# A hybrid mLSTM and neighbourhood-attention layer: key transposes spread over three steps, gate rows woven into a projection, eleven kinds of stores issued by ScalarE

## The chip, the core and the metric

The kernel runs on one core of a Trainium2 chip. The metric is the device time of one execution in microseconds, as the median of several runs. Before the change it is 1791.4 us (three runs: 1791.37, 1791.40, 1798.38).

## What is computed

One encoder layer over two sequences, a prompt of 512 tokens and a sample of 2048, each with 16 learned meta tokens in front, model width 1024, all in float32. RMS norm, one combined input projection, two branches with a SiLU gate each, one output projection into the residual. Branch A is a bidirectional mLSTM (4 heads of 128, one scan per direction), branch B neighbourhood attention over a grid of 64 columns (8 heads of 64, a window of 8 x 16 keys and the meta tokens). Cut to what matters here:

```python
def hybrid_layer(h, norm_g, w_in, b_gate, conv_w, mlstm_norm_g, q_norm_g, k_norm_g, rpb, w_out):
    proj = rms_norm(h, norm_g) @ w_in
    q_m, k_m, v_m, o_m, z_m, gates, q_a, k_a, v_a, z_a = jnp.split(proj, cuts, axis=-1)
    qk_m = silu(centred_dwconv(concatenate([q_m, k_m]), conv_w))
    h_m = mlstm_bidir(heads(q_m), heads(k_m), heads(v_m), gates + b_gate)
    h_m = rms_norm(sigmoid(heads(o_m)) * h_m, mlstm_norm_g)
    y_m = h_m * silu(z_m)
    qa, ka = rms_norm(heads(q_a), q_norm_g), rms_norm(heads(k_a), k_norm_g)
    a = neighbourhood_attention(qa, ka, heads(v_a), rpb)   # softmax over window and meta keys
    y_a = a * silu(z_a)
    return h + concatenate([y_m, y_a]) @ w_out
```

## The kernel before

Every projection is made of float32r matmuls of 128 x 128 weights: input and weight are split into a high and a low part, and three products are summed (`mm3`, L233 to L240; the tiles `mmt` and `mmf`). The 2560 tokens are worked off in two halves of 1280, each as blocks of 256, 512 and 512 tokens. A unit of work is 24 matmuls into a PSUM buffer of the pool `ps_mm`, which has two.

The program is a row of phases that are generators. `weave` (L923) runs one main generator and lets others go on by so many steps per step of the main one; `drain` runs one to its end. In turn:

- First half: `phase_a1` projects the attention's queries, keys and values (`qs`, `ks`, `vs` in HBM), `phase_a1_z` the attention's gate (`zs`), `phase_a2` the mLSTM's inputs (`kqs`, `vms`, `ozs`). Beside `phase_a2` the first attention runs, windows 1 and 2, at 0.3 steps per step.
- Second half: `phase_a1` with the rest of the first attention (0.6). Then `gate_rows` (L529): from the gates of all tokens it makes, for each of two directions, the scan's running sums and maxima, a chain of TensorE transposes, VectorE scans and ScalarE exponentials on tiles of 84 rows, all emitted at once. Then `phase_a1_z` with the second attention, windows 3, 4 and 0 (1.2), then `phase_a2` with the attention and the backward mLSTM states (`mlstm_back`).
- Last: `mlstm`, 20 chunks of 128 tokens, each with the output projection of an earlier chunk (`out_proj`, tile `ops`).

Attention goes by pairs of heads and windows (`AttPair`, L802). One pair has four steps (`attention`, L480). Tiles: `qt`, `kt`, `vt` are loaded; `qps` and `kps` are TensorE transposes of queries and keys, copied out as `Q` (VectorE) and `K` (ScalarE); `sps` are the scores, `s` their exponentials (VectorE adds the bias, ScalarE exponentiates), `pps` the transposes of `s`, copied out as `pt` (one by ScalarE, one by VectorE); `py` sums the values, `rb` is the transposed table of softmax reciprocals (`rx`, made by POOL), and `zt` = `rb` times gate times `py` is stored in `yas`. PSUM has four pools of two buffers: `ps_mm`, `ps_a` for `sps`, `ps_b` for `kps` and `pps`, `ps_c` for `qps`, `py`, `rb` and the gate rows' tiles.

Every DMA, load or store, is issued by SP, in order: an issue that waits holds all that stand behind it. `turn` (L163) fixes TensorE's order in the woven phases as emitted; the rest of the order is made by a scheduler when the program is built. Names of stores and lines: `qs`, `ks`, `vs` L340, `kmeta`, `vmeta` L300, `zs` L375, `kqs` L423 and L443, `vms`, `ozs` L456 and L474, `Mrow` L594, `cbs` L657, outputs L799, `yas` L920.

Of the kernel before, what the change touches and what calls it, by code (L numbers as in the profile page):

```python
# [92 lines left out]
class Run:  # L93
# [4 lines left out]
    def setup(self):  # L98
# [19 lines left out]
        nc.vector.memset(self.one, 1.0)  # L118

# [156 lines left out]
    def a1_meta(self, pool, gi, w, blk):  # L276
# [22 lines left out]
        for par in range(2):  # L299
            nc.sync.dma_start(out=dst[:, par::2, gi % 2 * 256:gi % 2 * 256 + 256], in_=raw[par * 8:par * 8 + 8].unsqueeze(1).to_broadcast([8, 4, 256]))  # L300
        yield

    def a1_tokens(self, pool, gi, n, w, blk):
# [4 lines left out]
        for t0 in range(0, blk["n"] // 128, 2):  # L308
# [36 lines left out]
    def phase_a1(self, blocks, pool, first=None):  # L345
# [3 lines left out]
        if first:  # L349
            g0 = 2  # L350
            for blk in blocks:
                for gi in range(2):
                    yield from self.a1_unit(pool, gi, self.A1[gi][1], first[gi], blk)
        for gi in range(g0, 6):
            c0, n = self.A1[gi]
            w = self.load_w(a["w_in"], c0, n)
            for blk in blocks() if callable(blocks) else blocks:
                yield from self.a1_unit(pool, gi, n, w, blk)

    def phase_a1_z(self, blocks, pool, done):  # L360

        nc, a = self.nc, self.a
        for gi in range(2):
            w = self.load_w(a["w_in"], 4112 + gi * 256, 256)
            for ct in range(2):
                for blk in blocks:
# [8 lines left out]
                    nc.sync.dma_start(out=self.zs[f:f + 128, blk["row0"]:blk["row0"] + n], in_=t[:, :n])  # L375
# [28 lines left out]
    def a2_conv(self, blocks, pool, c0, cbase, gi):  # L404
        nc, a, scr = self.nc, self.a, self.kqs
        w = self.load_w(a["w_in"], c0 + gi * 256, 256)
        for ct in range(2):
# [3 lines left out]
            for blk in blocks:  # L411
# [6 lines left out]
                if extra:  # L418
                    nc.vector.tensor_copy(out=self.mraw[:, cc, 4:4 + NM], in_=ps[:, n:n + NM])
                    if cbase == 4:  # L420
                        t = self.conv(pool, self.mraw[:, cc, :], 16, cc)
                        for sq in "PS":
                            nc.sync.dma_start(out=scr[sq][f:f + 128, 0:14], in_=t[:, 2:16])  # L423
# [19 lines left out]
                nc.sync.dma_start(out=scr[s][f:f + 128, o0:o0 + no], in_=t[:, :no])  # L443
                yield

    def a2_rows(self, blocks, pool, c0, kind, gi, free=None):
# [3 lines left out]
        for blk in blocks:  # L450
            if not blk["seq"]:
                if kind == "v":
# [3 lines left out]
                    nc.sync.dma_start(out=self.vms[2560:2560 + NM, dc:dc + 256], in_=buf[:NM])  # L456
# [4 lines left out]
            for t0 in range(0, blk["n"] // 128, 2):  # L461
# [12 lines left out]
                nc.sync.dma_start(out=dst[g0:g0 + 256, d0:d0 + 256].rearrange("(t p) c -> p t c", p=128), in_=buf.rearrange("p (t c) -> p t c", t=2))  # L474
# [5 lines left out]
    def attention(self, pool, wins, zdone):  # L480
# [3 lines left out]
        todo[0].prep(0)  # L484
        yield
        todo[0].prep(1)
        yield
        prev = None
        for n, p in enumerate(todo):
# [25 lines left out]
            if after:  # L515
                after.prep(1)
# [3 lines left out]
        yield  # L520
        yield
# [4 lines left out]
        prev.out()  # L526


    def gate_rows(self, pool):  # L529
# [4 lines left out]
        misc = pool.tile([128, 8, 128], F32, tag="kt", name="gmisc", bufs=2)  # L534
        zero, ones = misc[:NR, 0, :], misc[:NR, 1, :]
        nc.vector.memset(zero, 0.0)
        nc.vector.memset(ones, 1.0)
        self.cols = cp.tile([128, 2, 4, NR], F32, name="gcols")
        for d in range(2):
            big = pool.tile([128, 8, 128], F32, tag="vt", name=f"gbig{d}", bufs=2)  # L540
            mn, t, b, a, A, M, ws, ac = (big[:NR, i, :] for i in range(8))
            E = t
            row = misc[0:1, 2 + 3 * d:5 + 3 * d, :].rearrange("p a b -> p (a b)")[:, :4 * NR].rearrange("p (i r) -> p i r", i=4)
# [12 lines left out]
            nc.vector.tensor_tensor_scan(out=rv(A), data0=rv(a), data1=rv(zero), initial=-BIG, op0=ALU.max, op1=ALU.add)  # L556
            last = slice(127, 128) if d == 0 else slice(0, 1)
# [10 lines left out]
            for c0, nch in ((0, 4), (4, 16)):  # L568
# [25 lines left out]
            nc.sync.dma_start(out=self.Mrow[d].rearrange("(r j) -> r j", r=NR), in_=M)  # L594
# [10 lines left out]
            nc.vector.tensor_copy(out=cols[:, 3, :], in_=pd[:, 0:NR])  # L605

# [38 lines left out]
    def mlstm_back(self, pool, seq):  # L645
# [4 lines left out]
        for i in range(nch - 1, 0, -1):  # L650
# [6 lines left out]
            nc.sync.dma_start(out=self.cbs[c0 + i - 1], in_=C.rearrange("p h e -> p (h e)"))  # L657
# [104 lines left out]
    def load_wo(self, pool):  # L762
# [13 lines left out]
    def out_proj(self, seq, i, yh, yl):  # L776
# [22 lines left out]
        nc.sync.dma_start(out=ydst[i * 128:(i + 1) * 128, :], in_=x)  # L799


class AttPair:  # L802
# [9 lines left out]
    def load(self):  # L812
        nc, r, pool, nr, nk, f = self.nc, self.r, self.pool, self.nr, self.nk, self.f
        self.kt = pool.tile([128, 8, 128], F32, tag="kt", name="kt", bufs=2)
        self.vt = pool.tile([128, 8, 128], F32, tag="vt", name="vt", bufs=2)
# [9 lines left out]
    def prep(self, part):  # L825
# [10 lines left out]
        for half in range(2):  # L836
            ps = r.ps_b.tile([128, 512], F32, tag="t", name="kps")
            for c in range(4):
                r.turn(nc.tensor.transpose(ps[:, c * nk:(c + 1) * nk], self.kt[:nk, half * 4 + c, :], r.ident[:nk, :nk]))
            nc.scalar.activation(out=self.K[:, half * 4 * nk:(half + 1) * 4 * nk], in_=ps[:, :4 * nk], func=AF.Copy, scale=r.gk)  # L840

    def start(self):
        pool = self.pool
        self.py = self.r.ps_c.tile([128, 512], F32, tag="c", name="py")
# [3 lines left out]
    def scores(self, b):  # L848
        nc, r, pool, nk, n, bt = self.nc, self.r, self.pool, self.nk, 3 * self.nk, BTYPE[b]
        if bt not in self.bias:  # L850
            self.bias[bt] = pool.tile([128, 2, n], F32, tag="bias", name="bias", bufs=4)
# [8 lines left out]
        for hh in range(2):  # L860
            s = pool.tile([128, 384], F32, tag="s", name="s", bufs=6)
# [22 lines left out]
    def values(self, half):  # L884

        nc, r, nk, pts = self.nc, self.r, self.nk, self.pts.pop(half)
        order = ((1, 4, 0, 2, 3), (6, 3, 7, 5, 4))[half]
# [15 lines left out]

    def out(self):
# [240 lines left out]
```

## Time and profile before

| | before |
|---|---|
| median of three runs | 1791.4 us |
| the profiled execution | 1794.23 us |
| its span in the profile | 1792.5 us |
| TensorE matmul busy | 1693.5 us, 94% |
| VectorE busy | 906.5 us, 51% |
| ScalarE busy | 683.2 us, 38% |
| POOL busy | 405.3 us, 23% |
| mean granted TensorE clock | 0.983 |
| DMA, one queue (SP's) | 47.7% of 16 engines |

Busy times are unions over the span. Issues of DMAs and waits on semaphores count as idle. A matmul's end is modelled, so dense matmuls overlap in the listing: the distance between two starts is the pitch.

### The profile page before, as it was taken

To read this page: it belongs to the slowest core of one execution; us is meant where nothing else is said; L and a number is where in the kernel's file an instruction comes from. 1 tells how busy PE (TensorE), PEld (TensorE's weight loads), DVE (VectorE), ACT (ScalarE), POOL (GpSimd) and SP (SyncE) were. 2 spreads that over 40 slices of the span, in tenths; PEclk is the share of its full clock that TensorE was granted. 3 is DMA by queue.
4 is the path that set the end of the run, shared out by engine and by line. 5 is a ranking of instruction groups with operands and counts; after the bars stand their busy time and mean duration, and the time that the engine had idled before them with its cause. 6 is when DMAs were issued, how large, how long until landed. Compare 5 with 4: busy or idle time off the path is not lost. (4 is left out here: it accounts for less than half of the span.)

```text
span 1792.5 us, 32992 instructions
## 1 busy us (share of the span) xinstructions
PE 1693.5 (94%) x12476; PEld 1501.2 (84%) x12476; DVE 906.5 (51%) x2564; ACT 683.2 (38%) x1715; POOL 405.3 (23%) x383
## 2 busy tenths in 40 slices
PE   6999999999999989999799999999999899999899
PEld 6999988888989978998577777878888888877787
DVE  8896015253361266640334455353464378776662
ACT  5432223343342354222234445444444354543430
POOL 4021122221131231111011212211444232322210
PEclk9999999999999999999799999999999999999999
DMA  5466332333444554332454556754566666555431
GB/s 185 136 218 168 91 102 73 101 98 106 121 123 120 169 174 118 93 97 84 96 151 131 161 147 167 200 163 133 187 184 177 194 206 187 190 182 189 148 129 71
DMA packets 247166, 258.57 MB, mean 144 GB/s; under 512 B 17928, under 2 KB 204624, under 8 KB 247008
## 3 DMA queue, kind: packets, MB, share of 16 engines
q1 hardware_dynamic: 247008, 256.47, 47.7%
q8 instruction: 98, 1.61, 0.4%
q14 instruction: 60, 0.49, 0.1%
HBM read 183.05 MB, written 73.37 MB: 143 GB/s over the span
## 5 line engine op out<-in xcount | busy, mean ns | idle before, releaser
L239 PE MATMUL mmt<-wh,xah 128*128 128x256 f32 (+1 forms) x1536 | 438.9, 286 | 3.4 <-ACT mlo L260 3.4
L239 PE MATMUL mmt<-wl,xah 128*128 128x256 f32 (+1 forms) x1536 | 436.5, 284 | 1.4 <-POOL wl L230 1.4
L239 PE MATMUL mmt<-wh,xal 128*128 128x256 f32 (+1 forms) x1536 | 435.6, 284 | 0.0
L230 POOL TENSOR_TENSOR wl<-wr,wh 128x512 fp32r<-128x512 f32 (+1 forms) x184 | 247.3, 1357 | 700.0 <-ACT wh L229 691.9
L239 PEld LDWEIGHTS mmt<-wh,xah 128*128 128x128 f32 x1536 | 291.3, 190 | 4.7 <-ACT mlo L260 3.8
L239 PEld LDWEIGHTS mmt<-wl,xah 128*128 128x128 f32 x1536 | 290.8, 189 | 2.2 <-POOL wl L230 1.8
L239 PEld LDWEIGHTS mmt<-wh,xal 128*128 128x128 f32 x1536 | 292.3, 190 | 0.4 <-DVE xal L216 0.2
L387 DVE SCALAR_TENSOR_TENSOR acc<-craw,cw,acc 128x256 f32<-128x256 f32 (+2 forms) x192 | 147.1, 766 | 63.4 <-ACT acc L385 58.4
L229 ACT CAST wh<-wr 128x512 fp32r<-128x512 f32 (+1 forms) x184 | 110.1, 621 | 180.9 <-DMA wr<-in_w_in 135.1
L239 PE MATMUL mmf<-xah,wh 128*128 128x512 f32 x384 | 154.0, 401 | 3.0 <-ACT craw L431 1.5
L863 DVE CUSTOM_DVE_ANT_0 s<-sps,bias 128x384 f32<-128x384 f32 (+3 forms) x160 | 71.9, 483 | 161.7 <-PE sps L859 161.1
L239 PE MATMUL mmf<-xal,wh 128*128 128x512 f32 x384 | 152.0, 396 | 0.0
L239 PE MATMUL mmf<-xah,wl 128*128 128x512 f32 x384 | 151.6, 395 | 0.0
L239 PE MATMUL mmt<-wh,xbh 128*128 128x256 f32 (+1 forms) x384 | 112.3, 292 | 4.0 <-ACT xbh L215 2.7
L239 PE MATMUL mmt<-wl,xbh 128*128 128x256 f32 (+1 forms) x384 | 111.0, 289 | 0.0
L239 PE MATMUL mmt<-wh,xbl 128*128 128x256 f32 (+1 forms) x384 | 110.6, 288 | 0.4 <-DVE xbl L216 0.4
L864 ACT ACTIVATE s<-s,mx 128x384 f32<-128x384 f32 (+3 forms) x160 | 88.4, 555 | 22.0 <-DVE mx L863 21.4
L699 POOL TENSOR_TENSOR qw<-qw,kq 128x1024 f32<-128x1024 f32 (+1 forms) x20 | 63.4, 3168 | 131.9 <-ACT qw L698 121.8
L329 ACT COPY raw<-mmt 128x512 f32<-128x512 f32 x50 | 29.3, 585 | 159.1 <-PE mmt L239 152.3
L239 PEld LDWEIGHTS mmf<-xah,wh 128*128 128x128 f32 x384 | 72.6, 189 | 19.6 <-ACT craw L431 2.4
L373 DVE SCALAR_TENSOR_TENSOR zt<-zt,mmf 128x512 f32<-128x512 f32 (+1 forms) x24 | 14.4, 599 | 143.7 <-ACT zt L372 135.3
L239 PEld LDWEIGHTS mmf<-xah,wl 128*128 128x128 f32 x384 | 72.3, 188 | 17.2
(236 smaller groups left out, 3453.9 us busy)
## 6 DMA issues: line engine op xcount, KB each, us to landing
wr<-in_w_in SPq DMA_DIRECT2D x176, 256.0 KB
ozs<-vbuf SPq DMA_DIRECT2D x40, 256.0 KB
X<-Mrow SPq DMA_DIRECT2D x20, 512.0 KB
oz<-ozs SPq DMA_DIRECT2D x20, 512.0 KB
v<-vms SPq DMA_DIRECT2D x38, 256.0 KB
bias<-in_bias SPq DMA_DIRECT2D x24, 384.0 KB
x<-in_xs SPq DMA_DIRECT2D x16, 512.0 KB
kq<-kqsS SPq DMA_DIRECT2D x16, 512.0 KB
```

Of the source, the lines that this page charges most:

```text
L229: nc.scalar.copy(out=wh[:, ks, :n], in_=wr[:, :, :n])
L230: nc.gpsimd.tensor_tensor(out=wl[:, ks, :n], in0=wr[:, :, :n], in1=wh.bitcast(F32)[:, ks, :n], op=ALU.subtract)
L239: self.turn(nc.tensor.matmul(ps, st(s, k), mv(m, k), start=i == 0, stop=i == last))
L329: nc.scalar.copy(out=raw, in_=ps)
L373: nc.vector.scalar_tensor_tensor(out=t[:, :n], in0=t[:, :n], scalar=1.0, in1=ps[:, :n], op0=ALU.add, op1=ALU.mult)
L387: nc.vector.scalar_tensor_tensor(out=acc[:, :n], in0=raw[:, d:d + n], scalar=self.cw[:, ct, d:d + 1], in1=acc[:, :n], op0=ALU.mult, op1=AL ...
L699: nc.gpsimd.tensor_tensor(out=qw[:, :nd], in0=qw[:, :nd], in1=qT.unsqueeze(1).to_broadcast([128, nd, 4, 128]), op=ALU.mult)
L863: nc.vector.tensor_tensor_reduce(out=s[:, :n], in0=pss[hh][:, :n], in1=self.bias[bt][:, hh], op0=ALU.add, op1=ALU.min, scale=-1.0, scalar= ...
L864: nc.scalar.activation(out=s[:, :n], in_=s[:, :n], func=AF.Exp, scale=-1.0, bias=mx[:, 0:1], accum_out=self.sums[:, hh, b:b + 1])
```

## The change

Three parts. The key transposes of a pair (`prep`) come in two halves, and queries, first half and second half go to three steps, each at the head of its step; loads are issued a pair earlier (`vt` has three buffers, `bias` 3 instead of 4, `s` 4 instead of 6), `py` is allocated at its first product, and the reciprocals have a method of their own, `weights`, a step before `out`. `gate_rows` becomes a generator of five stages per direction, in tiles of another pool (`bp`), which starts when the first attention has ended and both gate projections are made, and goes on by 0.25 stages per step of `phase_a1`. Eleven kinds of stores are issued by ScalarE. The factor 0.5 of the attention's gate moves from `rx` into the weights `w_out`. Cut to its core:

```diff
+        self.zo = cp.tile([128, 2, 128], F32, name="zo")
+        nc.vector.memset(self.zo[:, 0, :], 0.0)
+        nc.vector.memset(self.zo[:, 1, :], 1.0)
+        self.gated, self.rested = 0, False
...
-                nc.sync.dma_start(out=dst[:, g0:g0 + 8, dc:dc + 256], in_=raw[half:half + 64, i // 2 * 256:i // 2 * 256 + 256])
+                nc.scalar.dma_start(out=dst[:, g0:g0 + 8, dc:dc + 256], in_=raw[half:half + 64, i // 2 * 256:i // 2 * 256 + 256])
...
-        todo[0].prep(0)
-        yield
-        todo[0].prep(1)
-        yield
+        for i in range(3):
+            todo[0].prep(i)
+            yield
+        todo[1].load()
...
             if after:
-                after.load()
-            yield
+                after.prep(0)
+            yield
+            if after:
+                after.prep(1)
             if prev:
                 prev.values(1)
             p.scores(1)
             p.probs(0)
-            yield
+            if prev:
+                prev.weights()
+            yield
+            if after:
+                after.prep(2)
             p.scores(2)
             p.probs(1)
-            if after:
-                after.prep(0)
             if prev:
                 while prev.pair not in zdone:
                     yield
                 prev.out()
+            if n + 2 < len(todo):
+                todo[n + 2].load()
             yield
             p.values(0)
             p.scores(3)
             p.probs(2)
-            if after:
-                after.prep(1)
             yield
...
     def gate_rows(self, pool):
+        while self.gated < 2 or not self.rested:
+            yield
+        zero, ones = self.zo[:NR, 0, :], self.zo[:NR, 1, :]
...
-            big = pool.tile([128, 8, 128], F32, tag="vt", name=f"gbig{d}", bufs=2)
-            mn, t, b, a, A, M, ws, ac = (big[:NR, i, :] for i in range(8))
+            big = [pool.tile([128, 4, 128], t) for t in ("kT", "v1")]
+            mn, t, b, a, A, M, ws, ac = (x[:NR, i, :] for x in big for i in range(4))
...
             nc.vector.tensor_tensor_scan(out=rv(A), data0=rv(a), data1=rv(zero), initial=-BIG, op0=ALU.max, op1=ALU.add)
+            yield
...
-            if k < 4:
-                nc.vector.tensor_scalar(out=wr, in0=wr, scalar1=self.mg[:, k:k + 1], scalar2=None, op0=ALU.mult)
+            nc.vector.tensor_scalar(out=wr, in0=wr, scalar1=self.mg[:, k:k + 1] if k < 4 else 0.5, scalar2=None, op0=ALU.mult)
...
+    def weights(self):
+        nc = self.nc
+        nc.vector.reciprocal(out=self.sums, in_=self.sums)
+        self.rx = self.pool.tile([128, 4, 2, 64], F32, tag="rx", name="rx", bufs=1)
+        nc.gpsimd.tensor_copy(out=self.rx, in_=view(self.sums[:, 0, 0:1], [[1, 4], [4, 2], [0, 64]]))
...
-    weave(R.phase_a1(blocks2, ap), (att, 0.6), (rl, 3))
+    gates = R.gate_rows(bp)
+    weave(R.phase_a1(blocks2, ap), (att, 0.6), (rl, 3), (gates, 0.25))
     drain(att)
+    drain(gates)
     R.last = False
-    R.gate_rows(tp)
```

The order shows what moves. First TensorE at the border of the second half's `phase_a1` and `phase_a1_z` (`gpr`, `gpc`, `gpt`, `gpd` are PSUM tiles of the gate rows). Before, the first direction's rows, behind the first block of the gate projection `mmf`:

```order
L239 MATMUL mmf<-xbh,wl 128x256
L560 MATMUL gpr<-ident,gbig_9869 1x84
L561 MATMUL gpr<-ident,gbig_9869 1x84
L581 MATMUL gpc<-one,gmisc 84x1
L582 MATMUL gpc<-one,gmisc 84x1
L597 MATMUL gpt<-ident,gbig_9869 128x84 x3
L598 MATMUL gpt<-ident,gcol 1x84
L604 MATMUL gpd<-gmisc,one 128x84
L547 MATMUL gps<-ident,gates 84x128
```

Now, one of the stages, inside the projection of keys:

```order
L243 MATMUL mmt<-wl,xah 128x256
L243 MATMUL mmt<-wh,xal 128x256
L612 MATMUL gpt<-ident,v_8674 128x84 x2
L612 MATMUL gpt<-ident,kT 128x84
L613 MATMUL gpt<-ident,gcol 1x84
L243 MATMUL mmt<-wh,xah 128x256
```

The gate rows stood in one block of both directions; now each stage has 64 or some 97 matmuls of the projection between itself and the next.

Second, TensorE in a step of the second attention. Before, between two units of projection matmuls, `rb` of the pair that ends and then the last step of the pair that runs:

```order
L916 MATMUL rb<-ident,rx 128x128 x4
L901 MATMUL py<-pt,vt 64x128 x2
L901 MATMUL py<-pt,vt 64x64 x4
L901 MATMUL py<-pt,vt 64x128 x2
L901 MATMUL py<-pt,vt 64x192 x2
L901 MATMUL py<-pt,vt 64x128 x2
L859 MATMUL sps<-K,Q 64x384 x4
L876 MATMUL pps<-ident,s 128x128 x6
L839 MATMUL kps<-ident,kt 128x104 x8
```

Now:

```order
L243 MATMUL mmf<-xah,wl 128x512
L854 MATMUL kps<-ident,kt 128x128 x4
L873 MATMUL sps<-K,Q 64x384 x4
L890 MATMUL pps<-ident,s 128x128 x6
L934 MATMUL rb<-ident,rx 128x128 x4
L243 MATMUL mmf<-xbh,wh 128x256
```

The eight `kps` behind `pps` are two groups of four ahead of `sps`, and `rb` has a unit of projection matmuls behind it where `py` stood.

Third, ScalarE's queue in the second half's `phase_a1` beside the first attention. Before:

```order
L324 COPY raw<-mmt 128x256
L325 ACTIVATE sq<-mmt 128x256
L880 COPY pt<-pps 128x3x128
L864 ACTIVATE s,sums<-s,mx 128x384 x2
```

Now:

```order
L1065 CAST xah<-xre 128x512
L344 DMA qs<-raw 8x8x256 x4
L328 COPY raw<-mmt 128x256
L329 ACTIVATE sq<-mmt 128x256
L878 ACTIVATE s,sums<-s,mx 128x384
L894 COPY pt<-pps 128x3x128
```

Four stores of `qs` stand ahead of the copy of the next unit; they wait for VectorE's `raw` of an earlier one.

## Rows read from the trace of the kernel before

**Rows 1.** The page, busy time of each engine, share of the span, instructions.

```profile
PE 1693.5 (94%) x12476; PEld 1501.2 (84%) x12476; DVE 906.5 (51%) x2564; ACT 683.2 (38%) x1715; POOL 405.3 (23%) x383
```

**Rows 2.** Waits, whole span: who waited for whom, us in total, times, longest.

```profile
PE xps L210 <- DVE x L207: 12.2, 5, 8.3
PE kps L839 <- ACT pt L880: 8.6, 18, 2.7
PE kps L839 <- DVE pt L882: 7.6, 5, 2.6
PE py L901 <- DVE zt L918: 5.8, 7, 1.1
...
PE sps L859 <- ACT K L840: 2.1, 1, 2.1
...
ACT qw L698 <- DMA X<-Mrow: 60.0, 16, 6.0
```

**Rows 3.** Windows around the gate rows: length, busy by engine, granted clock, DMA.

```profile
846.76:870.18 23.42, 7.43 (x30) 4.65 (x31) 13.56 (x59) 8.35 (x16) 3.23 (x3) 0.61 0.34 95
870.18:872.60 2.42, 2.42 (x8) 1.94 (x7) 0.75 (x1) 0.00 (x0) 0.00 (x0) 0.51 0.95 220
```

**Rows 4.** Windows, stretches of low clock in the attention steps.

```profile
647.30:654.10 6.80, 4.23 (x20) 3.83 (x20) 6.70 (x23) 4.10 (x9) 3.15 (x3) 0.50 0.55 186
...
906.30:914.00 7.70, 5.62 (x37) 4.79 (x36) 1.72 (x6) 4.58 (x11) 4.01 (x3) 0.78 1.05 252
```

**Rows 5.** Timeline at the first gate transposes: start, us, engine, line, operation.

```profile
843.42 0.28 PE L239 MATMUL mmt<-wh,xal 128*128 128x256 f32 x1
843.55 0.27 PE L547 MATMUL gps<-ident,gates 128*84 128x128 f32 x1
843.66 0.27 PE L548 MATMUL gps<-ident,gates 128*84 128x128 f32 x1
...
849.31 0.41 DVE L556 TENSOR_TENSOR_SCAN gbig<-gbig,gmisc 84x128 f32<-84x128 f32 x1
```

**Rows 6.** Timeline, TensorE in steps of the second attention.

```profile
957.59 0.60 PE L916 MATMUL rb<-ident,rx 128*128 128x128 f32 x4
958.97 1.43 PE L901 MATMUL py<-pt,vt 128*64 128x128 f32 x24 [0.78 <-DVE zt L918]
960.34 0.88 PE L859 MATMUL sps<-K,Q 64*64 64x384 f32 x8
...
963.74 1.09 PE L839 MATMUL kps<-ident,kt 128*128 128x128 f32 x8 [1.72 <-ACT pt L880]
```

**Rows 7.** Windows, the second projection of keys and values.

```profile
717.00:761.80 44.80, 44.80 (x392) 44.45 (x391) 27.32 (x92) 11.67 (x23) 8.64 (x7) 1.00 0.33 93
```

**Rows 8.** Line L840, the copy of the keys: duration min/median/max in ns.

```profile
L840 ACT ACTIVATE K<-kps,gk x40: 478/591/692, 310.9 to 1226.6; 128x512 f32<-128x512 f32 x16, 128x384 f32<-128x384 f32 x8, 128x416 f32<-128x416 f32 x8, 128x288 f32<-128x288 f32 x8
```

**Rows 9.** Lines L340 and L799, issues on SP: duration min/median/max in ns.

```profile
L340 SPq DMA_DIRECT2D qs<-raw x80: 570/575/639, 38.1 to 736.6; - x80
...
L799 SPq DMA_DIRECT2D out_s<-xres x16: 337/338/351, 1452.6 to 1740.6; - x16
```

**Rows 10.** Waits of SP's queue, whole span.

```profile
SPq L799 <- DVE xres L798: 113.4, 15, 13.3
SPq L443 <- DVE ct L389: 97.7, 32, 7.1
...
SPq L340 <- DVE raw L336: 68.1, 27, 5.4
```

**Rows 11.** Timeline, the second projection of queries: SP's stores, a gap of ScalarE.

```profile
664.84 2.53 SPq L340 DMA_DIRECT2D qs<-raw  x4
...
681.35 0.37 ACT L324 COPY raw<-mmt 128x256 f32<-128x256 f32 x1 [2.87 <-DVE qrt L181]
```

**Rows 12.** Timeline of SP in one chunk of the last phase.

```profile
1543.91 0.34 SPq L799 DMA_DIRECT2D out_s<-xres  x1
...
1556.44 0.39 SPq L691 DMA_DIRECT2D X<-Mrow  x1
```

More of the change, by code (lines that the diff above doesn't have):

```diff
@@ L299, in a1_meta @@
         for par in range(2):
-            nc.sync.dma_start(out=dst[:, par::2, gi % 2 * 256:gi % 2 * 256 + 256], in_=raw[par * 8:par * 8 + 8].unsqueeze(1).to_broadcast([8, 4, 256]))
+            nc.scalar.dma_start(out=dst[:, par::2, gi % 2 * 256:gi % 2 * 256 + 256], in_=raw[par * 8:par * 8 + 8].unsqueeze(1).to_broadcast([8, 4, 256]))
         yield
@@ L374, in phase_a1_z @@
                     f = (gi * 2 + ct) * 128
-                    nc.sync.dma_start(out=self.zs[f:f + 128, blk["row0"]:blk["row0"] + n], in_=t[:, :n])
+                    nc.scalar.dma_start(out=self.zs[f:f + 128, blk["row0"]:blk["row0"] + n], in_=t[:, :n])
                     yield
@@ L422, in a2_conv @@
                         for sq in "PS":
-                            nc.sync.dma_start(out=scr[sq][f:f + 128, 0:14], in_=t[:, 2:16])
+                            nc.scalar.dma_start(out=scr[sq][f:f + 128, 0:14], in_=t[:, 2:16])
                 raw = pool.tile([128, 518], F32, tag="b", name="craw", bufs=5)
@@ L442, in a2_conv @@
                 o0 = NM + blk["t0"] - 2
-                nc.sync.dma_start(out=scr[s][f:f + 128, o0:o0 + no], in_=t[:, :no])
+                nc.scalar.dma_start(out=scr[s][f:f + 128, o0:o0 + no], in_=t[:, :no])
                 yield
@@ L455, in a2_rows @@
                     self.sum_m(pool, buf[:NM], ps, slice(0, 256))
-                    nc.sync.dma_start(out=self.vms[2560:2560 + NM, dc:dc + 256], in_=buf[:NM])
+                    nc.scalar.dma_start(out=self.vms[2560:2560 + NM, dc:dc + 256], in_=buf[:NM])
                     yield
@@ L473, in a2_rows @@
                 g0 = blk["row0"] + t0 * 128
[L474 removed]
+                nc.scalar.dma_start(out=dst[g0:g0 + 256, d0:d0 + 256].rearrange("(t p) c -> p t c", p=128), in_=buf.rearrange("p (t c) -> p t c", t=2))
                 if free and t0 + 2 == blk["n"] // 128:
@@ L520, in attention @@
         yield
+        prev.weights()
         yield
@@ L593, in gate_rows @@
             nc.vector.tensor_scalar(out=M, in0=M, scalar1=mp, scalar2=None, op0=ALU.subtract)
-            nc.sync.dma_start(out=self.Mrow[d].rearrange("(r j) -> r j", r=NR), in_=M)
+            nc.scalar.dma_start(out=self.Mrow[d].rearrange("(r j) -> r j", r=NR), in_=M)
+            yield
             pt = self.ps_c.tile([128, 512], F32, tag="c", name="gpt")
@@ L656, in mlstm_back @@
             C = new
-            nc.sync.dma_start(out=self.cbs[c0 + i - 1], in_=C.rearrange("p h e -> p (h e)"))
+            nc.scalar.dma_start(out=self.cbs[c0 + i - 1], in_=C.rearrange("p h e -> p (h e)"))
             yield
@@ L798, in out_proj @@
             nc.vector.tensor_tensor(out=x[:, cs], in0=ps, in1=x[:, cs], op=ALU.add)
-        nc.sync.dma_start(out=ydst[i * 128:(i + 1) * 128, :], in_=x)
+        nc.scalar.dma_start(out=ydst[i * 128:(i + 1) * 128, :], in_=x)
 class AttPair:
@@ L835, in prep @@
             return
[L836 to L840, printed above, removed]
+        half = part - 1
+        ps = r.ps_b.tile([128, 512], F32, tag="t", name="kps")
+        for c in range(4):
+            r.turn(nc.tensor.transpose(ps[:, c * nk:(c + 1) * nk], self.kt[:nk, half * 4 + c, :], r.ident[:nk, :nk]))
+        nc.scalar.activation(out=self.K[:, half * 4 * nk:(half + 1) * 4 * nk], in_=ps[:, :4 * nk], func=AF.Copy, scale=r.gk)
     def start(self):
         pool = self.pool
-        self.py = self.r.ps_c.tile([128, 512], F32, tag="c", name="py")
         self.sums = pool.tile([128, 2, 4], F32, tag="sums", name="sums", bufs=2)
@@ L850, in scores @@
         if bt not in self.bias:
-            self.bias[bt] = pool.tile([128, 2, n], F32, tag="bias", name="bias", bufs=4)
+            self.bias[bt] = pool.tile([128, 2, n], F32, tag="bias", name="bias", bufs=3)
             nc.sync.dma_start(out=self.bias[bt], in_=r.a[f"bias{self.wt}"][self.pair, bt])
@@ L886, in values @@
         nc, r, nk, pts = self.nc, self.r, self.nk, self.pts.pop(half)
+        if self.first:
+            self.py = r.ps_c.tile([128, 512], F32, tag="c", name="py")
         order = ((1, 4, 0, 2, 3), (6, 3, 7, 5, 4))[half]
@@ L919, in out @@
         nc.vector.tensor_tensor(out=zv, in0=pv(self.py), in1=zv, op=ALU.mult)
-        nc.sync.dma_start(out=r.yas[self.f, cols], in_=zt)
+        nc.scalar.dma_start(out=r.yas[self.f, cols], in_=zt)
 def weave(main, *others, until=None):
```

22 lines of the change are left out of this document (10 added, 12 removed).

## The prediction

> **What bounds the kernel now.** I read the page's busy shares first [rows 1]. TensorE is busy 94% of the span, the next engine (VectorE) 51%, ScalarE 38%, so the time can fall in only two ways: TensorE waits less, or it runs its clock at the full level for longer. The page leaves 1792.5 - 1693.5 = 99.0 us in which TensorE does nothing. The list of TensorE's waits says what ended that idle time [rows 2]. Four kinds of entry belong to places that the change touches: the eight-fold key transposes `kps` (8.6 + 7.6 = 16.2 us), the value products `py` (5.8 us), the scores `sps` behind the copy of the keys (2.1 us), and the gate rows `gpr`, `gpc`, `gpt`, `gpd`. The others (`yps`, `xps`, `ups`) stand in code that the change leaves as it is. Nothing in that list is a wait of TensorE for a load of weights or keys that is worth counting.
>
> The table by windows then shows the gate rows as one hole [rows 3]: from 846.76 to 870.18 us TensorE issues 30 matmuls and is busy 7.43 of 23.42 us, at a granted clock of 0.61. The stretch before it is dense at full clock. Behind it the clock is at 0.51, which is the lower of its two levels (1.2 instead of 2.4 GHz), for 2.42 us more, and then back at 1.00. Further stretches with a low clock stand where TensorE has just waited in the attention steps: one of 6.8 us at 0.50, and two of 3.4 us, one of which brings the window around 910 us down to 0.78 [rows 4].
>
> **The change part by part.**
>
> *Gate rows.* They leave their place between the two phases and go, one stage at a time, between projection matmuls. The order shows about 97 matmuls of the key and value projection between stages (64 once). At about 0.12 us each (843.42 to 843.55, [rows 5]) that is some 11 us, or 7.5 us for the short one. The chain of one stage is shorter: from `gps` at 843.66 to the end of the second scan at 849.72 the old run took 6.1 us, an activation-table load and another phase's work included. So each stage's result is there when TensorE comes to it. What TensorE keeps is the work itself: 30 matmuls less the four `qps` are 26; a gate transpose among dense matmuls costs 0.11 us (843.55 to 843.66, [rows 5]), so 26 x 0.11 = 2.9 us; the `qps` cost 0.6 us like four other transposes at full clock [rows 6]. The low clock behind the hole costs between nothing and half of its 2.42 us; I take the middle, 0.6. Term: 23.4 - 2.9 - 0.6 + 0.6 = **20.5 us** saved. From both sides: 21 if the clock's share is larger; 14 if each of six waits of the new places sticks out by 1 us. I take 20.5, because VectorE, which carries the chain, is idle for 17.5 of 44.8 us there, and ScalarE for 33 [rows 7].
>
> *Key transposes in two halves, ahead of the scores.* Before, eight transposes stand right behind six `pps` transposes, and their two PSUM buffers are those that `pps` has just filled; so the first half waits for ScalarE's copy and the second for VectorE's (1.72 us before one group of eight, [rows 6]). Now each half opens its step, behind a unit of projection matmuls, when both buffers have long been read: the 16.2 us [rows 2] lose their cause. A smaller one takes its place: the second `pps` buffer must now wait until ScalarE has read `kps` (0.59 us, [rows 8]), while TensorE has `sps` (0.88 us) and the first half of `pps` to do in between. With ScalarE free that hides; with ScalarE 0.3 us late it does not. Ends: 16.2 and 4 saved. I take **10**, nearer the upper end, since the cover is 1.3 us against 0.6.
>
> *`py` allocated late, `rb` placed apart.* The 5.8 us arise because `py` follows `rb` directly and needs the buffer that VectorE is still reading (0.78 us in [rows 6]). In the second attention phase the order now has a projection unit between them. Ends: 5.8 and 0; I take **5**. The `sps` wait of 2.1 us occurs once, at the start of the second attention, where `sps` came straight after the eight `kps`; now a unit lies between. I take **1**.
>
> *Clock.* In the stretch of 6.8 us TensorE is busy 4.23 us at half speed, so some 2 us are lost; by the same share the two of 3.4 us lose about 1 us each [rows 4]. They come behind waits that mostly go. Ends 5 and 0; I take **3**.
>
> *Stores from ScalarE.* 450 stores leave SP: 240 of `qs`, `ks`, `vs` at 0.575 us, and 210 others at about 0.34 [rows 9], some 138 + 71 = 209 us of issue time, put on an engine busy 683 us [rows 1]. Each also waits on ScalarE for its producer, mostly VectorE, and holds what stands behind it. The trace has no store on ScalarE. From below: nothing, since ScalarE is idle 62% of the span and mostly waits for TensorE's next product. From above: the whole issue time in two places. In the second projection, 10 groups of four `qs` stores take 2.5 us each, while a gap of ScalarE there is 2.9 us [rows 11], and others are shorter: 10 x 1 us. In the last phase 20 output stores of 0.34 us [rows 9]: 6.8 us. And 1 us for the rest (conv stores, `cbs`). I take **+7 us** of an upper end of 18: the projection's two PSUM buffers absorb a late copy of a few microseconds.
>
> *What the loads gain.* SP no longer waits 113 us for `xres`, 98 for `ct`, 68 for `raw` [rows 10]. I count nothing for it, because TensorE's list has no such wait. The Trainium skill, "DMA: Bandwidth & Descriptors", section "Issuing engines are not separate DMA queues", speaks against this part: engines that issue share the same 16 DMA engines, and a second issuer saves only the first one's issue time. By that rule the sum stays as it is. At the head of the program `x` loads stand behind `qs` stores on SP. TensorE waits there 12.2 us for `xps` [rows 2], of which 8.3 is the very first; that bounds a gain by 3.9 us.
>
> *Small edits.* The four added scalings of `wor` lie on VectorE, beside projection work and long before the first product that needs them. Fewer `bias` and `s` buffers cost nothing: the scores of the next pair come after the transposes that free them, in TensorE's own order. `rx` is made one step earlier, on POOL, for which nobody waits.
>
> **Sum**: 20.5 + 10 + 5 + 1 + 3 - 7 = 32.5 us off the profiled execution's own 1794.2 us, that is 1761.7. That execution lies 2.8 us above the median of the runs, 1791.4; so I forecast a median of **1759 us**, 1.8% less.
>
> **The rivals.**
>
> *The wait moves (1774 us).* Only the gate rows pay. The new `pps` behind `K` takes what `kps` gives back, `py` gains little, the stores cost what I took: 20.5 + 4 - 7 = 17.5 off, 1794.2 - 17.5 - 2.8 = 1774. For it: the attention steps are a relay between TensorE, VectorE and ScalarE, and ScalarE gets more to do. Against it: a projection unit of 24 matmuls stands in most steps.
>
> *ScalarE is held by its stores (1799 us).* About 190 stores or groups wait for a VectorE result; ScalarE is strictly in order, and exponentials, PSUM copies and `K` stand behind. If TensorE loses 0.25 us for each, that is 47 us against 39.5 saved: 1794.2 + 7.5 - 2.8 = 1799. It decides from 0.21 us a group. For it: SP spent 113, 98 and 68 us waiting for just these producers [rows 10]. Against it: SP came to them early because it had nothing else to do; in the order the stores stand behind the next unit's copies, when VectorE is done.
>
> *The freed queue is worth much (1729 us).* In the last phase the chain runs through the load of `X` (ScalarE's `qw` waits 60.0 us for it in 16 cases, [rows 2]), and if SP issued it 2 us earlier in 15 chunks, 30 us more would go: 1759 - 30. Against it: there `X` is issued at 1556.44, directly behind `oz`, `kq` and `CBl`, and the store went out at 1543.91, 12.5 us earlier [rows 12]; what holds `X` is the load of `oz`, which waits for `hs` and stays on SP. The rule of the skill cited above agrees, and this trace with it.
>
> That the change does not do what it says is excluded by the order: the stores stand on ScalarE, and the gate rows between projection matmuls.
>
> **How the numbers follow.** Forecast 0.62, wait moved 0.25, ScalarE held 0.07, freed queue 0.06. The likeliest case gives 1759. The low end: gate 21, `kps` 16, `py` 6, clock 5, `sps` 2, head 4, no cost of stores: 54 off, 1737. The high end: gate 14, `kps` 4, `py` 2, nothing from the clock, stores 12: 8 off, 1783. Between them lie the forecast and the second case; outside, the third and fourth and the tails, together below 2 in 10. 0.5% is about what a measurement of this kernel can tell from no change; that is 9 us, so faster means below 1782.4: the forecast, nearly all of the second case and the fourth, 0.88; same 0.07; slower 0.05.
>
> **What would show it.** In the profile after: no stretch near 850 us with a granted clock of 0.61, and gate matmuls with idle time under 2 us in all; the `kps` group's idle time below 3 us, and `pps` with a new entry behind `K` of not more than 6; no entry of `py` behind `zt` in the second attention; ScalarE busy as before, with stores on its queue, SP with loads and spills alone. I am wrong if `pps`, `sps` or `mmt` show long waits for ScalarE work that itself sat behind a store, or if the gate matmuls wait in their new places.

## The result and the profile after

The changed kernel takes **1765.7 us** (median of four runs, 1762.55 to 1775.35); the kernel before took 1793.9 beside it. The ratio is 0.9849 with a 95% interval of 0.9804 to 0.9894: 1.5% faster. Forecast were 1759 (1.8%) and a range of 1737 to 1783. The medians differ by 28.2 us, where the forecast had 32.4. The profiled execution took 1762.55 us, 31.7 less than that of before; the sum of the prediction was 32.5, but part of that agreement is luck, since this execution was the fastest of its four. One execution of e7 below took 3767.11 us and is left out of its row.

The page's busy times and the line on the core, which answer to [rows 1] and the table of before:

```profile
PE 1681.4 (95%) x12476; PEld 1498.6 (85%) x12476; DVE 913.3 (52%) x2568; ACT 680.3 (39%) x1715; POOL 388.2 (22%) x383
core 0: 1760.8 us, clock 0.990
```

TensorE issues the same 12476 matmuls and is busy 12.1 us less; idle it is 1760.8 - 1681.4 = 79.4 us instead of 99.0, which is 19.6 less. The busy part goes with the clock: a mean granted clock of 0.983 over 1792.5 us leaves 30.5 us of full clock ungranted, 0.990 over 1760.8 us leaves 17.6, and the difference of 12.9 is about those 12.1.

The waits after, those of TensorE first and then two of ScalarE (engine, line, for whom: us in total, times, longest), against [rows 2]:

```profile
PE pps L890 <- ACT K L855: 8.2, 9, 1.8
...
PE mmt L243 <- ACT craw L437: 4.1, 2, 3.3
PE mmt L243 <- ACT sq L335: 3.9, 3, 1.9
...
PE mmt L243 <- ACT raw L333: 1.0, 1, 1.0
...
PE py L917 <- DVE pt L896: 0.5, 1, 0.5
...
PE kps L854 <- ACT pt L894: 0.2, 1, 0.2
...
ACT raw L333 <- DMA ks<-raw: 31.2, 7, 6.7
...
ACT qw L714 <- DMA X<-Mrow: 61.4, 16, 5.8
```

The 16.2 us at `kps` and the 5.8 at `py` are gone, no gate row is in the list, and three things are new: `pps` waits 8.2 us behind the copy of the keys, the projection (`mmt`) waits for `sq` and `raw` (the copy of a unit out of PSUM and its square, both made by ScalarE), and ScalarE stands 31.2 us behind `ks` stores on its own queue.

Windows of the changed kernel (length; busy PE, PEld, DVE, ACT, POOL; granted clock; DMA share; GB/s). The first two lie in the first projection, the last two where the gate rows went and where they had been:

```profile
130.00:160.00 30.00, 28.14 (x231) 27.94 (x230) 22.49 (x73) 7.74 (x16) 5.78 (x5) 0.97 0.54 154
160.00:190.00 30.00, 27.80 (x227) 27.32 (x227) 11.40 (x39) 5.94 (x12) 5.81 (x5) 0.98 0.40 116
744.00:792.00 48.00, 48.00 (x405) 47.60 (x404) 34.83 (x139) 15.83 (x31) 5.76 (x5) 1.00 0.36 94
844.00:874.00 30.00, 30.00 (x190) 25.73 (x192) 4.56 (x10) 7.73 (x16) 5.12 (x4) 1.00 0.48 137
```

The hole of [rows 3] is closed: TensorE is busy for all of 844 to 874 at full clock, and dense at 744 to 792 with gate matmuls in between. In the first projection, which neither gate rows nor attention touch, 4.06 of 60 us are idle. The kernel before was busy for all 60:

```profile
130.00:160.00 30.00, 30.00 (x257) 30.00 (x256) 24.95 (x85) 7.67 (x15) 6.41 (x5) 1.00 0.59 156
160.00:190.00 30.00, 30.00 (x256) 30.00 (x255) 9.79 (x26) 6.77 (x13) 5.82 (x5) 1.00 0.55 149
```

The first Tanh behind that projection, ScalarE's first work in the gate projection, starts at 225.8 us before and at 233.1 after: 7.3 us are lost by then. In the profiles below it starts at 225.8 to 227.9 us where all stores stand on SP, and at 231.3 to 234.6 where all stand on ScalarE in the change's order. The last product of the output projection starts 31.7 us earlier than before.

### The profile page after: what moved, and what is told of

It reads as the page before. It is cut to its first block, busy times and chain, and to the rows that moved or that the text cites. A ratio compares the mean times of both kernels' runs of the same rounds, so it can differ in the third digit from the quotient of the medians.

```text
span 1760.8 us, 32817 instructions
## 1 busy us (share of the span) xinstructions
PE 1681.4 (95%) x12476; PEld 1498.6 (85%) x12476; DVE 913.3 (52%) x2568; ACT 680.3 (39%) x1715; POOL 388.2 (22%) x383
## 5 line engine op out<-in xcount | busy, mean ns | idle before, releaser
L393 DVE SCALAR_TENSOR_TENSOR acc<-craw,cw,acc 128x256 f32<-128x256 f32 (+2 forms) x192 | 154.6, 805 | 84.4 <-ACT acc L391 78.5
L878 ACT ACTIVATE s<-s,mx 128x384 f32<-128x384 f32 (+3 forms) x160 | 88.7, 557 | 31.7 <-DVE mx L877 16.8
L890 PEld LDWEIGHTS pps<-ident,s 128*128 128x128 f32 (+3 forms) x480 | 48.5, 130 | 53.6 <-issue 21.9
L379 DVE SCALAR_TENSOR_TENSOR zt<-zt,mmf 128x512 f32<-128x512 f32 (+1 forms) x24 | 14.4, 599 | 151.1 <-ACT zt L378 146.8
```

What stands on the lines that cost most here:

```text
L393: nc.vector.scalar_tensor_tensor(out=acc[:, :n], in0=raw[:, d:d + n], scalar=self.cw[:, ct, d:d + 1], in1=acc[:, :n], op0=ALU.mult, op1=AL ...
L878: nc.scalar.activation(out=s[:, :n], in_=s[:, :n], func=AF.Exp, scale=-1.0, bias=mx[:, 0:1], accum_out=self.sums[:, hh, b:b + 1])
L890: r.turn(nc.tensor.transpose(pp[:nk, j * 128:(j + 1) * 128], s[:, j * nk:(j + 1) * nk], r.ident))
```

## The experiments

The column "busy" is TensorE's time in the two windows of the first projection (of 60 us), "Tanh" the start of the first one behind it, in each one's profiled execution. Ratios are to the kernel before, with 95% intervals; compare by them, since the runs were made on several chips (e1, e3, e4 and e9 to e11 on one, e5 to e8 on a second, e12 and e13 on a third, each beside its own runs of before).

| run | stores from | median us | ratio | busy | Tanh |
|---|---|---|---|---|---|
| before | SP | 1793.9 | 1 | 60.0 | 225.8 |
| whole change | ScalarE | 1765.7 | 0.9849 (0.9804 to 0.9894) | 55.9 | 233.1 |
| e1 gate rows alone | SP | 1776.0 | 0.9884 (0.9861 to 0.9907) | 60.0 | 227.3 |
| e3 stores alone | ScalarE | 1800.2 | 1.0015 (1.0002 to 1.0028) | 55.7 | 233.3 |
| e4 whole, stores on SP | SP | 1754.4 | 0.9758 (0.9739 to 0.9777) | 60.0 | 226.2 |
| e5 attention alone | SP | 1774.5 | 0.9875 (0.9853 to 0.9897) | 60.0 | 227.8 |
| e6 whole again | ScalarE | 1771.4 | 0.9849 (0.9824 to 0.9875) | 56.0 | 234.6 |
| e7 `qs`, `ks`, `vs` on SP | both | 1758.9 | 0.9786 (0.9758 to 0.9814) | 59.2 | 228.3 |
| e8 these a unit later | ScalarE | 1764.0 | 0.9807 (0.9782 to 0.9833) | 57.9 | 229.4 |
| e9 as e4 | SP | 1756.4 | 0.9764 (0.9739 to 0.9789) | 60.0 | 227.9 |
| e10 as e4, `K` by VectorE | SP | 1753.4 | 0.9760 (0.9733 to 0.9787) | 60.0 | 226.9 |
| e11 stores by GpSimd | POOL | 1763.3 | 0.9803 (0.9780 to 0.9827) | 60.0 | 228.5 |
| e12 attention and stores | ScalarE | 1781.3 | 0.9902 (0.9881 to 0.9923) | 55.0 | 232.5 |
| e13 gate rows and stores | ScalarE | 1789.4 | 0.9947 (0.9931 to 0.9964) | 56.0 | 231.3 |

### The three parts, one at a time

e1 takes the kernel before and changes the gate rows alone:

```diff
+        while self.gated < 2 or not self.rested:
+            yield
...
-    R.gate_rows(tp)
+    weave(R.phase_a1(blocks2, ap), (att, 0.6), (rl, 3), (gates, 0.25))
```

> The kernel before with the woven gate rows alone (their generator, their tiles, the 0.25 in the weave; the score buffers s go from 6 to 4 for room, as in the whole change). Theory: the gate rows' place was a hole of 23.4 us in which TensorE was busy 7.4 and the clock low, so this part alone gives some 20 us, about 1774 from 1794, and the first Tanh of the second z phase comes some 20 us earlier against the end of the projection ahead of it. Rival (the hole only moves): the six waits of the new places, or the chain of VectorE behind the projections, stick out; then the gain is 10 us or less, 1784 or more, and the waits of TensorE name gpr, gpc or gpt.

0.9884 of 1797.7, the median of before in that session, is **20.9 us** less. No `gpr`, `gpc` or `gpt` is left in TensorE's waits; the `kps` and `py` entries stay about as before (9.6 + 8.1 and 5.0). The Tanh that the expectation names was the wrong sign to look for: it stood ahead of the old gate rows. The last Tanh of that phase is what comes some 20 us earlier, at 938.4 against 958.6 us.

e5 changes the attention steps alone (`attention`, `AttPair`, the 0.5 in `load_wo`):

> The kernel before with the new attention steps alone (key transposes in three steps, the value products' bank taken late, the weights made ahead of out, loads two pairs ahead, the 0.5 in the output weights; gates and stores as before, the scratch of the gates in the three vt buffers). Theory: the parts add up. The whole change with its stores on SP stood at 1754.4 and the gate rows alone gave 21.7 of 1797.7, so the attention steps alone give 21 to 22, about 1776, and the wait of the probability transposes behind the copy of the keys is there at some 8 us, as it is with the stores on either engine. Rival: the steps pay only together with the woven gate rows, since the second attention starts on a warm clock only then; under 14 us here, 1784 or more. Second rival: the 8 us behind the key copy need a busier ScalarE and are under 3 here.

0.9875 is **22.5 us**. The new wait is there with ScalarE free of stores, in e5's list of waits:

```profile
PE pps L879 <- ACT K L844: 8.6, 9, 1.8
```

So it belongs to the steps, and not to the stores. Both rivals fall. The forecast here was made by subtraction, with e1 and e4 known; before that, for a run of the same steps that gave no result (e2), 13 us had been expected, with the whole 8 us of the `pps` wait taken off.

e3 moves the eleven kinds of stores alone:

```diff
-                nc.sync.dma_start(out=dst[:, g0:g0 + 8, dc:dc + 256], ...
+                nc.scalar.dma_start(out=dst[:, g0:g0 + 8, dc:dc + 256], ...
```

> The kernel before with all eleven kinds of stores issued by ScalarE and nothing else. Theory: ScalarE holds the copies that free the projection's two banks behind stores that wait for VectorE, so it is slower by some 7 us, about 1801 from 1794, nearly all of it before the first Tanh of the first z phase (225.8 us into the run before, 233 with the whole change). Rival (the queue with loads alone pays): the loads of the last phase start earlier, and it is faster by 3 us or more, 1791 or less, with fewer microseconds behind 1400. Second rival: the whole change's loss in the first projection is a matter of that one execution; then this is within 3 us of before, and the first Tanh comes before 229 us.

It is slower by 0.15%, 2.7 us (0.4 to 5.0), less than the theory said and as little as the second rival had; but the place is the theory's (Tanh at 233.3, 55.7 of 60 us busy). e4 is the reverse, the whole change with `nc.sync` in all eleven places:

> The whole change with all its stores issued by SP again. Theory: the 7 us of the first projection come back, and the last phase keeps its gain of 3 us or less, so about 1759 to 1762 where the whole change had 1765.7; the waits of mmt for sq, raw and craw on ScalarE fall from some 12 us to under 4. Rival: the loads need the queue for themselves once the steps are closer together; then it is 1770 or more, with new waits for loads.

> The variant with all stores on SP once more, beside the next two on one chip. All theories expect 1752 to 1758 (1754.4 before).

e4 was faster than the theory had it, e9 fell into its band: 0.9758 and 0.9764 against 0.9849. TensorE's waits of `mmt` for `sq`, `raw` and `craw` fall from 9.0 us to 1.9. **The stores on ScalarE cost the change 0.0088 of 1797.7, 15.8 us**, with an interval of some 5 us to either side. The order that the scheduler makes moves with the stores and is part of that figure. Without them gate rows and attention add up: 20.9 + 22.5 = 43.4, measured 43.5 and 42.4. e6 asks whether the distance is one of chips:

> The whole change once more, on the chip of the variants it is compared with. All theories expect 1764 to 1768; a figure at 1755 would mean that its distance of 11 us to the variant with the stores on SP was one of chips.

Its median came out above the band, and its before is higher too (1798.7 against 1793.9); the ratio is the same to four digits. No run has the whole change and the variant of e4 side by side on one chip; but the medians of before on three chips lie between 1797.7 and 1800.5 us, so on the old kernel these chips differ by less than 3 us.

The profiles show where the price falls (start in us; two executions of each):

| | stores on SP (e4, e9) | on ScalarE (whole change, e6) | mean difference |
|---|---|---|---|
| first Tanh of the first gate projection | 226.2, 227.9 | 233.1, 234.6 | 6.8 |
| first Tanh of the second | 842.3, 844.0 | 851.6, 855.3 | 10.3 |
| first output product | 1397.3, 1397.5 | 1406.0, 1416.3 | 13.8 |
| last output product | 1746.3, 1748.4 | 1756.0, 1769.0 | 15.2 |

Nearly half is lost by the end of the first projection; the last phase itself loses 1.4.

### Why the old kernel hid the stores' price

The stores cost 2.7 us in the old kernel and 15.8 in the new one. Two runs ask which part makes them dearer:

> The kernel before with the new attention steps and the stores on ScalarE, the gate rows as before. It tells where stores on ScalarE cost more: they took 2.7 us of the old kernel (ratio 1.0015) and some 16 of the new one (0.9849 against 0.9758 and 0.9764). If it is the new attention steps that make them dearer (more of ScalarE's work is then waited for at once: K ahead of pt), this stands 12 us or more above the attention steps alone (0.9875), at 0.994 or more of before. If each part adds its own, it stands some 3 us above them, at 0.989 or 0.990.

> The kernel before with the woven gate rows and the stores on ScalarE, the attention steps as before. If it is the woven gate rows that make the stores dearer, this stands 12 us or more above the gate rows alone (0.9884), at 0.995 or more of before; if each part adds its own, at 0.990 or so. If neither this nor the run beside it shows more than 6 us, the excess needs all three parts, or lies in the spread of the runs.

Above the attention steps they add 0.0027 (5 us), above the gate rows 0.0063 (11 us), just under the 12 us that the expectation had set. By the intervals the second is clear of the old kernel's 0.0015, the first is not. So it is mainly the old place of the gate rows that makes stores look cheap. TensorE's waits at the gate rows show how. In the kernel before they are 15.8 us:

```profile
PE gpr L560 <- DVE gbig L554: 4.8, 2, 3.4
PE gpc L581 <- DVE gmisc L577: 4.3, 1, 4.3
PE gpr L561 <- DVE gbig L556: 1.9, 2, 1.4
PE gpt L597 <- DVE gcol L586: 1.7, 2, 0.8
PE gpc L581 <- DVE gmisc L579: 1.6, 1, 1.6
PE gpd L604 <- DVE gmisc L602: 1.5, 2, 0.7
```

In e3:

```profile
PE gpr L560 <- DVE gbig L554: 5.0, 1, 5.0
PE gpc L581 <- DVE gmisc L579: 1.6, 1, 1.6
PE gpr L561 <- DVE gbig L556: 1.1, 1, 1.1
PE gpt L597 <- DVE gcol L586: 0.8, 1, 0.8
PE gpd L604 <- DVE gmisc L602: 0.7, 1, 0.7
```

9.2 us, and each wait once. With the stores moved, the scheduler set the first pair of gate transposes at 764.4 us, inside the projection (843.5 before), so half of the hole went as a side effect; in e12 the same (764.5 us, waits of 8.0). That pays back 6.6 us of waits and some of the clock (the stretch at 0.5 shrinks from 20.5 to 13.7 us). Where the rows are woven there is nothing to pay back, and the price stands bare. How far the stores on ScalarE set back the two ends of the second gate projection, at whose head the old gate rows stand, tells the same (one profile each):

| stores moved in | its first Tanh, us | its last |
|---|---|---|
| the old kernel (before, e3) | 12.7 later | 5.5 later |
| with the new attention steps (e5, e12) | 14.4 | 5.4 |
| with the woven gate rows (e1, e13) | 9.6 | 11.2 |
| with both (e4, whole change) | 9.3 | 9.1 |

### Wait, issue or other stores

e7 puts the `qs`, `ks` and `vs` stores back on SP; e8 leaves them on ScalarE and issues those of one unit where the next unit's stood:

```diff
+            self.flush()
+            self.pend = (dst, raw, (blk["row0"] // 64 + t0 * 2) * 8, dc)
```

> The whole change with only the qs, ks and vs stores (240 of the 450) back on SP. Theory: the loss is all in these, because they go out four at a time on the engine that frees the projection's banks; 1754 to 1757, as with all stores on SP, and the first Tanh of the first z phase near 226 us instead of 233. Rival: the other 210 stores carry their share (210 of 450 of the 11 us, some 5 us); 1759 or more. Third case: SP with fewer stores gains where all stores on SP cost; below 1752.

> The whole change, stores on ScalarE, but the four qs, ks or vs stores of a unit are issued one unit later, when VectorE has long scaled them. Wait theory: what holds ScalarE is the 3.6 us in which VectorE makes the scale (147.84 to 151.47 in the trace of the whole change), which with 1.1 us of copies and 2.5 of issue is 7.2 us against a unit of 5.7 on TensorE; without that wait 3.6 us of 5.7 are left and the first projection loses nothing: the first Tanh of the z phase at 226 to 228, the time 1756 to 1759. Issue theory: what holds it is the issue itself, which took 5.06 us for four at 151.55, while SP issued loads, instead of 2.45; that stays, the first Tanh comes at 231 or later and the time is 1762 or more.

e7 stands between its first two cases, close to the second (1758.9, Tanh at 228.3): these 240 stores cost 0.9849 - 0.9786 = 0.0063, 11 us, and some 4.5 us are left for the other 210, which the intervals don't separate from nothing. e8 stands between its theories by its Tanh (229.4), and by its time, 1764.0, in the band of the issue theory. Against e6, beside which it ran, it gets back 0.0042 of those 0.0063, 7.5 us (with some 6 to either side), without any store leaving ScalarE. So most of the figure goes with **the place of the stores in ScalarE's order**. That does not part waiting from issuing cleanly, since in e8 the issues are less drawn out as well (four took at most 3.3 us between 140 and 170 us, where the whole change has the 5.06). What e8 still loses in the first projection (2.1 of 60 us) stands in its list of waits, for 130 to 162 us:

```profile
ACT raw L334 <- DMA kmeta<-rawm: 9.7, 1, 9.7
```

The line names only the last of what stood there. From 139.45 us on ScalarE waited for VectorE's `raw` (142.37 to 143.04) of four stores that were already put off by a unit, issued them until 145.77, and then waited for the `kmeta` stores, which I had not put off and which follow a VectorE chain as well (issued 147.60 to 149.05). So one unit was not always late enough. In 160 to 190 us e8 loses nothing (30.00 of 30).

The timeline of ScalarE in the whole change shows the mechanism (start, length, engine; "ACTq" is an issue). What ended a wait is inferred in the listing: the last line names a load, but `sq` does not read it, and what stands ahead of `sq` are the four issues.

```profile
146.72 0.59 ACT L333 COPY raw<-mmt 128x512 f32<-128x512 f32 x1 [4.46 <-DVE qry L186]
147.20 0.62 ACTq L344 DMA_DIRECT2D ks<-raw  x1
147.21 0.60 ACT L335 ACTIVATE sq<-mmt 128x512 f32<-128x512 f32 x1
147.86 2.99 ACTq L344 DMA_DIRECT2D ks<-raw  x3
150.94 0.59 ACT L333 COPY raw<-mmt 128x512 f32<-128x512 f32 x1 [3.13 <-DMA ks<-raw]
151.55 5.06 ACTq L344 DMA_DIRECT2D ks<-raw  x4
156.65 0.60 ACT L335 ACTIVATE sq<-mmt 128x512 f32<-128x512 f32 x1 [5.12 <-DMA qt<-qs]
```

and VectorE beside it:

```profile
147.84 0.69 DVE L337 TENSOR_REDUCE ss<-sq 128x8 f32<-128x512 f32 x1 [0.67 <-ACT sq L335]
...
150.78 0.69 DVE L340 TENSOR_TENSOR raw<-raw,qry 128x512 f32<-128x512 f32 x1
...
157.28 0.69 DVE L337 TENSOR_REDUCE ss<-sq 128x8 f32<-128x512 f32 x1 [5.81 <-ACT sq L335]
```

A unit is a ring: ScalarE copies and squares (1.1 us), VectorE makes the scale and applies it (147.84 to 151.47, 3.6 us), ScalarE issues four stores (2.5 us at best). Where the stores stand ahead of the next unit's square, the ring is run in series, 7.2 us, while TensorE fills a PSUM buffer in 48 matmuls of 0.12, 5.7 us. Here VectorE was done at 151.47, and the issue that began at 151.55 took 5.06 us more. The square of the next unit came at 156.65, 5.7 us behind its copy, VectorE's next chain with it, and TensorE waited for the buffer. On SP the same stores hold nothing that TensorE waits for (60.0 of 60 us busy in e4 and e9).

The ring does not cost at every unit. The values have no scale, so the four stores of a unit wait for no other engine. They take the same 2.5 us for four, and TensorE loses nothing beside them:

```profile
190.00:220.00 30.00, 30.00 (x256) 30.00 (x255) 0.00 (x0) 5.85 (x11) 5.78 (x5) 1.00 0.41 108
```

That is evidence for waiting over issuing from the change's own profile. The queries have the ring too, and from 70 to 130 us TensorE loses nothing there either (60.00 of 60): the loss stands in the keys, and why not in the queries was not tried.

### What loads alone on SP are worth

> The whole change with its eleven kinds of stores issued by GpSimd instead of ScalarE: SP's queue has loads alone, as in the change, and ScalarE none of the stores. It tells what loads alone on SP are worth. Theory: nothing, since SP without stores only stands longer before loads whose buffers are not free (344 us for wr in the whole change, 149 with the stores on SP) and ScalarE's wait for X stayed at 61 us; so at best 1754 as with the stores on SP, and more by what the stores hold up on GpSimd (weight remainders, qw), 1754 to 1775. Rival (loads alone pay, ScalarE's load hid it): 1750 or less.

ScalarE has no stores here and TensorE loses nothing in the first projection (60.0 of 60 us), SP has loads alone, and the first output product starts at 1394.4 us, against 1397.5 in e9. Behind that product time is lost: from 1430 to 1670 TensorE is busy 225.46 us where e9 has 230.36, where GpSimd makes `qw` and `al` and now issues stores between them (whether that is the cause was not tried apart). The time, 1763.3 us, is the theory's and not the rival's. SP's own longest wait, in the whole change, in e4 and in e11:

```profile
SPq L232 <- POOL wl L234: 344.1, 131, 20.0
```

```profile
SPq L232 <- POOL wl L234: 149.2, 109, 5.6
```

```profile
SPq L232 <- POOL wl L234: 376.3, 126, 20.2
```

Freed of stores, SP comes to the next load sooner and stands there until its buffer is free. ScalarE's wait for `X` was 60.0 us before and is 61.4, 62.1 and 67.0 in these three. The Trainium skill, "DMA: Bandwidth & Descriptors", section "Issuing engines are not separate DMA queues", says that a second issuer saves only the time in which a DMA is started. These runs agree: what was saved was time that SP had.

### The new wait behind the keys

In e4, at the longest of these waits, ScalarE does this:

```profile
956.73 0.62 ACT L233 CAST wh<-wr 128x512 fp32r<-128x512 f32 x1 [0.85 <-DMA wr<-in_w_in]
957.25 0.60 ACT L855 ACTIVATE K<-kps,gk 128x416 f32<-128x416 f32 x1
```

The copy of the keys stands behind a cast of weights whose load had not landed. So it is in three of e4's nine waits, the longest, 4.9 of 8.7 us; in the other six ScalarE came to `K` late by copies and casts of its own that waited for no load. e10 gives the copy to VectorE:

```diff
-        nc.scalar.activation(out=self.K[...], in_=ps[:, :4 * nk], func=AF.Copy, scale=r.gk)
+        nc.vector.tensor_scalar(out=self.K[...], in0=ps[:, :4 * nk], scalar1=r.gk, scalar2=None, op0=ALU.mult)
```

> All stores on SP, and the copy of the transposed keys (K out of kps) on VectorE instead of ScalarE. Theory: the probability transposes wait 8.7 us behind that copy because ScalarE reaches it late: at 956 it stood 0.85 us in a cast of weights whose load had not landed, with K behind it, while VectorE had nothing to do for 3 us. On VectorE the entry behind K falls under 3 us and the time by 4 to 8 us, to 1747 to 1751. Rival (the wait moves again): VectorE has the mask sums of the scores and the convolutions in its queue, the transposes wait for K or for pt on VectorE instead, or sps for mx; then the waits of TensorE in these steps add up to as much as before and the time is within 3 us of the run beside it.

In e9, the run beside it:

```profile
PE pps L890 <- ACT K L855: 7.9, 9, 1.8
...
PE ups L653 <- ACT kw L643: 3.3, 2, 2.9
```

In e10:

```profile
PE ups L653 <- ACT kw L643: 5.5, 6, 2.8
...
PE pps L890 <- DVE K L855: 1.9, 2, 1.0
```

The entry falls from 7.9 us in e9 to 1.9, while `ups` behind `kw` rises from 3.3 to 5.5. The medians are 1753.4 and 1756.4, the ratios 0.9760 and 0.9764: a gain of 3 us is not resolved, and the theory's 4 to 8 are not borne out; the rival's time is.

## Why the prediction was right, and where it was off

The mechanism was right for the gate rows, right in the main for the attention steps, and wrong for the stores. The total came out near, in part by luck: a price of the stores that was 8.8 us too low, against a gain of the attention steps that was 3.5 too low, though within its interval. Measured, the parts are 20.9 + 22.5 - 15.8 = 27.6 us, and the whole 27.1 (0.0151 of 1797.7); forecast were 20.5 + 19 - 7 = 32.5.

- **Gate rows**, 20.5 forecast, 20.9 alone (16.7 to 25.0). The hole closed, no wait moved into the projection, and the low clock there went with it.
- **Key transposes, `py`, `sps` and clock**, 10 + 5 + 1 + 3 = 19, measured 22.5 with an interval of 18.5 to 26.4. `kps` went to 0.2 us, `py` to 0.5. The `pps` wait, "with ScalarE free that hides", took 8.2 us where I had set at most 6; by the waits alone that leaves 7.8 of the 10 us that I had put. Its cause was not a ScalarE late by stores: e5 has it too. In e4, for over half of it, a cast that waited for its weights stood in front of `K`; for the rest it was other work of ScalarE. So the first rival's wait came, and not its price: the time was made good elsewhere in these steps, by how much each the runs don't tell.
- **Stores**, +7 of an upper end of 18, measured +15.8. This is the term that failed. The step was "in the order the stores stand behind the next unit's copies, when VectorE is done". They stood ahead of the next unit's square; the order that I had printed for the second half has four `qs` stores ahead of the next unit's copy, too. And nearly half of the price fell in the first projection, which I had not looked at: I read gaps of ScalarE in the second [rows 11], and had put 6.8 us of the upper end into the last phase, which lost 1.4. The rival of a ScalarE held by its stores had the form right, and its price, 47 us, was three times too large.
- **Loads**: nothing counted, nothing found. The freed queue gave the last phase no earlier `X`, as [rows 12] said.
- Of what the profile was to show, only the bound on `pps` was broken; `mmt` waiting for work behind a store was named as a sign of error, and is there, in `sq` and `raw` (4.9 us in four waits).

**The faster version** is the change without its third part: stores on SP (e4, e9), 0.976 of before, ahead of the whole change by 0.9%.

## What to carry to other kernels

Before moving a store to a compute engine, write down the ring it joins: what that engine made, who must answer, and what stands behind the store; if the ring run in series is longer than the bound engine's unit, it can cost time, however idle the engine looks on the whole. Here it did so in the keys. An issuer that waits long before its stores is no bottleneck if nothing that is waited for stands behind them. And measure a part beside its fellows: in the old kernel, gate rows that the scheduler moved hid most of the stores' price.

## What was not expected

Four stores on ScalarE took 5.06 us from 151.55 on, though each issue lasts 0.59; eight took the same 5.06 from 161.61 on. In the first stretch SP was issuing loads, in the second nearly none:

```profile
151.94 1.36 SPq L838 DMA_DIRECT2D qt<-qs  x2
153.34 0.55 SPq L835 DMA_DIRECT2D kt<-ks  x1
153.94 0.74 SPq L836 DMA_DIRECT2D kt<-kmeta  x1
154.72 1.52 SPq L838 DMA_DIRECT2D qt<-qs  x2
158.81 1.30 SPq L866 DMA_DIRECT2D bias<-in_bias  x3
```

ScalarE's four issues start at 151.55, 153.75, 154.73 and 156.02, each close to the end of one or two of SP's. It looks as if two issuers take turns, so that a busy SP stretches ScalarE's stores. The stores at this place are drawn out in e6 as well (eight from 148.8 us on took 9.06), but no run tested the cause.
